# A feed-forward on Trainium2 in seven block products for eight over two token groups

## The chip, the cores and the metric

The kernel runs on one core of a Trainium2 chip. Its time is the device time of one execution in microseconds; the kernel before takes 1440.34 us (median of 3 runs, 1440.0 to 1440.73).

## What is computed

One layer for 8 samples of one token and a prompt of 1024 tokens: a mixer, attention over a memory, and a feed-forward, each added to the residual x. The change touches the feed-forward alone, with 1024 features and 4096 hidden ones, in fp32:

```python
D_MODEL, D_FF = 1024, 4096
def rmsnorm(x, g):
    xf = x.astype(jnp.float32)
    y = xf * lax.rsqrt(jnp.mean(xf * xf, axis=-1, keepdims=True) + EPS)
    return (y * g.astype(jnp.float32)).astype(x.dtype)
def ffn(x, g, w1, w2):
    h = rmsnorm(x, g) @ w1
    return jnp.square(jax.nn.relu(h)) @ w2
...
        xp = xp + mem_attend(xp, mk, mv, g_mem_x[l], mem_w_q[l], mem_g_q[l], mem_w_o[l])
        xp = xp + ffn(xp, g_ffn[l], ffn_w1[l], ffn_w2[l])
```

## The kernel before, in words

The 1032 tokens lie along the free axis in three groups of GW = 344 columns, samples first; the features lie on the partitions, 128 to a tile. XT[m] is the residual, in eight tiles. An fp32 product is made of three products in a rounded type: each operand is split into a rounded half and what is left (`halves`: a copy on ScalarE, ACT, and a subtraction on VectorE, DVE), and `dense` adds wh xh, wh xl and wl xh in PSUM on TensorE (PE).

Weights come in staged halves of 128x512 (ws, by DMAs that the queue of SyncE, SP, issues) and are split into wh and wl (`Blk`, `feed`). The framework's scheduler sets the order of every engine's queue when the program is built: by the order of the code, with splits ranked 50 instructions earlier (LIFT_W) and what empties an accumulator 600 earlier (LIFT_E). At run time each engine works through its queue in order and waits where an operand or a buffer isn't ready.

The feed-forward runs in six chunks of 6, 6, 5, 5, 5, 5 hidden tiles (CHUNKS). `ffn_up(j)` makes one hidden tile over the three groups (`f1_cell`: 24 products, then DVE multiplies max(x, 0) by 1/rms from rbf, ACT squares, ACT and DVE split into fhl). `ffn_down` takes for each of the eight output tiles m the chunk's hidden tiles (3 products each and group) and DVE adds the sum into XT[m]; in the last chunk `y_out(m)` transposes and stores the tile. The factor 1/rms is thus applied behind the products: the halves XH and XL of x carry only the gain (`norm_halves`, in `o_cell`). POOL (GpSimd) adds up the squares for the norm (`norm_sum`) and has no work afterwards. The first cells of the feed-forward stand in the code beside the memory's output products of groups 1 and 2 (`o_cells`, `up_cell`), where the streams of the memory attention run too.

Of the kernel before, what the change touches and what calls it, by code (L numbers as in the profile page):

```python
# [10 lines left out]
F32 = mybir.dt.float32  # L11
# [20 lines left out]
# SBUF slots by tag: floats per partition, count  # L32
# [11 lines left out]
# by stream: a handicap (ns) when the next one is chosen, and how much earlier its instructions rank  # L44
# [8 lines left out]
def trunk_step(ctx: ExitStack, tc: tile.TileContext, I: dict, O: list):  # L53
# [95 lines left out]
    # Ln and Tanh lie in different tables: they keep their order, with a load where they alternate  # L149
# [60 lines left out]
    def rsqrt(out, ss, scale, tmp):  # L210
        """out = (ss * scale + eps) ** -0.5, with one Newton step; tmp: a spare like out, or already the base"""
# [26 lines left out]
    def release(tag, key=None, n=1):  # L238
        """a slot is free again; with a key: once n have said so"""
# [129 lines left out]
    def halves(hi, lo, src):  # L369
        """hi = src rounded, lo = what is left"""  # L370
# [1569 lines left out]
```

## Time and profile before

| | |
|---|---|
| median of 3 runs | 1440.34 us |
| profiled execution, its span | 1436.8 us |
| PE busy | 1381.1 us (96%) |
| DVE, ACT, POOL busy | 745.2, 560.2, 101.6 us |
| DRAM read, written | 84.49 MB, 6.65 MB |

For the profiled execution the span is the only time on record: from its first to its last instruction, 3.5 us below the median of the runs. The busy times are sums over the whole span; where an engine's share is read for one stage, the table by stages is used. PE's products overlap, so their spacing, not the length of one record, tells what one costs.

### The profile page before, as it was taken

How to read it: one execution, taken by the hardware profiler on the slowest of the kernel's cores; microseconds unless marked ns; L12 is line 12 of the kernel's file. 1: busy time of each engine (PE TensorE's matmuls, PEld its weight loads, DVE VectorE, ACT ScalarE, POOL GpSimd, SP SyncE). 2: the span in 40 equal slices, each digit the busy share in tenths (PEclk: the TensorE clock that was granted, in tenths of full speed). 3: DMA queues.
4: the chain of work that ended last, by engine and by line, in shares of the span. 5: the costliest groups of instructions: out<-in, count | busy, mean ns of one | idle time of the engine just before them, and what ended most of it. 6: DMA issues, size and time to landing. Idle time of an engine off the chain costs nothing.

```text
span 1436.8 us, 22961 instructions
## 1 busy us (share of the span) xinstructions
PE 1381.1 (96%) x9029; PEld 1277.6 (89%) x9029; DVE 745.2 (52%) x1716; ACT 560.2 (39%) x1183; POOL 101.6 (7%) x137
## 2 busy tenths in 40 slices
PE   6999999999996899998899999999999999999998
PEld 5899888787886877877799999999999999999998
DVE  6276888477668664767843333333333333333331
ACT  5265465256475554565642123113212212312321
POOL 3001012300003101121300000000000000000000
PEclk9999999999997999998999999999999999999999
DMA  6014021211003444422221121111111111112032
GB/s 194 30 48 126 3 47 32 57 31 45 23 8 101 139 143 136 120 75 75 81 81 45 52 60 34 45 56 40 36 57 54 32 58 51 35 52 60 29 88 70
DMA packets 164692, 91.58 MB, mean 64 GB/s; under 512 B 24322, under 2 KB 159606, under 8 KB 164568
## 3 DMA queue, kind: packets, MB, share of 16 engines
q1 hardware_dynamic: 163944, 89.81, 21.7%
q8 instruction: 71, 1.16, 0.3%
q0 software_dynamic: 640, 0.30, 0.1%
q14 instruction: 37, 0.30, 0.1%
HBM read 84.49 MB, written 6.65 MB: 63 GB/s over the span
## 4 chain that ended last, share of the span: by engine, by line
PE 82%; DVE 10%; ACT 3%; DMA 3%; issue 1%; POOL 0%; SPq 0%; ACTq 0%; DVEq 0%; POOLq 0%
PE f L140 49%; PE win L140 8%; PE wo L140 6%; PE v L140 2%; PE gx L140 2%; PE wmo L140 1%; PE mx L140 1%; PE rgp L140 1%; DVE wl L170 1%; DMA ws<-in_w_in_dram 1%; PE go L140 1%; PE mpo L140 1%; DVE XL L181 1%; PE wq L140 1%; PE sx L140 1%
## 5 line engine op out<-in xcount | busy, mean ns | idle before, releaser
L140 PE MATMUL f<-fhl,wh 128*128 128x344 f32 x1536 | 364.8, 320 | 0.0
L160 ACT ACTIVATE wh<-ws 128x512 fp32r<-128x512 f32 (+2 forms) x292 | 159.7, 578 | 433.0 <-PE f L140 361.2
L140 PEld LDWEIGHTS f<-fhl,wh 128*128 128x128 f32 x1536 | 264.9, 188 | 0.0
L140 PE MATMUL f<-XH,wh 128*128 128x344 f32 x768 | 246.8, 321 | 2.5 <-DVE nrm L181 1.4
L140 PE MATMUL f<-XH,wl 128*128 128x344 f32 x768 | 245.6, 320 | 0.0
L140 PE MATMUL f<-fhl,wl 128*128 128x344 f32 x768 | 245.4, 320 | 0.0
L140 PE MATMUL f<-XL,wh 128*128 128x344 f32 x768 | 244.9, 319 | 0.0
L170 DVE TENSOR_TENSOR XT<-XT,f 128x344 f32<-128x344 f32 x144 | 73.8, 512 | 246.1 <-PE f L140 246.1
L170 DVE TENSOR_TENSOR wl<-ws,wh 128x512 fp32r<-128x512 f32 (+2 forms) x292 | 178.5, 639 | 31.9 <-ACT wh L160 27.4
L140 PEld LDWEIGHTS f<-XH,wh 128*128 128x128 f32 x768 | 144.4, 188 | 3.6 <-ACT wh L160 3.0
L140 PEld LDWEIGHTS f<-XH,wl 128*128 128x128 f32 x768 | 144.3, 188 | 0.3 <-issue 0.2
L140 PEld LDWEIGHTS f<-XL,wh 128*128 128x128 f32 x768 | 144.1, 188 | 0.4
L140 PEld LDWEIGHTS f<-fhl,wl 128*128 128x128 f32 x768 | 144.2, 188 | 0.0
L140 PE MATMUL win<-XL,wh 128*128 128x344 f32 x384 | 126.6, 330 | 0.0
L140 PE MATMUL win<-XH,wh 128*128 128x344 f32 x384 | 126.2, 329 | 0.2 <-ACT xy L160 0.2
L140 PE MATMUL win<-XH,wl 128*128 128x344 f32 x384 | 125.4, 327 | 0.0
L181 DVE SCALAR_TENSOR_TENSOR nrm<-f,rbf 128x344 f32<-128x344 f32 x96 | 49.4, 516 | 143.4 <-PE f L140 143.2
L160 ACT ACTIVATE nrm<-nrm 128x344 f32<-128x344 f32 x99 | 48.1, 487 | 159.1 <-DVE nrm L181 159.1
L170 DVE TENSOR_TENSOR fhl<-nrm,fhl 128x344 fp32r<-128x344 f32 x96 | 49.6, 517 | 68.6 <-ACT fhl L160 66.8
L140 PEld LDWEIGHTS win<-XL,wh 128*128 128x128 f32 x384 | 72.2, 188 | 5.2 <-issue 3.9
L140 PEld LDWEIGHTS win<-XH,wl 128*128 128x128 f32 x384 | 72.3, 188 | 3.6 <-issue 2.7
L140 PEld LDWEIGHTS win<-XH,wh 128*128 128x128 f32 x384 | 72.2, 188 | 3.3 <-issue 1.9
(427 smaller groups left out, 2105.8 us busy)
## 6 DMA issues: line engine op xcount, KB each, us to landing
ws<-in_ffn_w_dram SPq DMA_DIRECT2D x124, 256.0 KB
ws<-in_w_in_dram SPq DMA_DIRECT2D x24, 256.0 KB
ws<-in_w_out_dram SPq DMA_DIRECT2D x24, 256.0 KB
x<-in_x_prompt_dram SPq DMA_DIRECT2D x8, 512.0 KB
xr<-in_x_prompt_dram SPq DMA_DIRECT2D x16, 256.0 KB
out_dram<-yo SPq DMA_DIRECT2D x8, 512.0 KB
ws<-in_w_out_dram SPq DMA_DIRECT2D x24, 128.0 KB
ws<-in_w_out_dram SPq DMA_DIRECT2D x48, 64.0 KB
```

Source lines behind the costliest of these rows:

```text
L140: PE.matmul(out, lhsT, rhs, start=start, stop=stop)
L160: return ACT.activation(out, in_, func, **kw)
L170: return DVE.tensor_tensor(out, a, b, op=op)
L181: DVE.scalar_tensor_tensor(out, a, s, b, op0=op0, op1=op1, **kw)
```

## The change

The feed-forward is cut into 2x2 blocks of weights and two blocks of tokens (groups 0 and 1), and each 2x2 by 2x2 product is done with seven block products for eight, in Winograd's form of Strassen's method; group 2 is done in the plain way beside it, with the same weights. Sums of weight blocks (S1 to S4) and of operand blocks (T1 to T4) are made before the products and split afterwards; sums of results (U, V) behind them.

- Hidden tiles go in 16 pairs of 256. The first two pairs are plain (`pl_cell`, 12 cells of 24 products). The other 14 are `up_unit`s, 132 products each for 144.
- All of the way up comes first. Of each pair `h_done` makes nine operands (B11, B21, T1 to T4, B22, and GA, GB2 of group 2), `h_store` splits each and stores both halves to DRAM (hd): 352 KB an operand. T1, T2, T3 and T4 are sums on POOL.
- The way down is 16 `down_unit`s (8 steps of 512 hidden features by 2 halves of the output), 132 products each for 144. `h_load` fetches the operands of step c+1 while step c runs.
- `x_ready(g)` now normalises x (gain and 1/rms) before the products and splits it. `x_ops` makes T1 to T4 of x, even feature tiles on DVE, odd ones on POOL.
- XT goes to DRAM (`x_spill`) for the way up and comes back (`x_fill`), so that its place is free.
- Weights come raw (`unit_raw`, 1 MB a unit); `unit_sums` makes S1 to S4 on POOL, `prep` splits one of the eight weight operands of a unit, LOOK = 5 operands ahead of its use.
- `y_out` stands for four output tiles in the unit before the last and for four in the last one.

```diff
...
-            for k in {6: (), 7: (6, 7)}.get(m, (m,)):
-                norm_halves(k, g, GFF)
             norm_sum(m, g, NRM["f"])
+        if m == 7 and g == 0:
+            x_ready(0)
+
+    def x_ready(g):
+        with lift(LIFT_E):
+            norm_end(g, NRM["f"])
+            for m in range(8):
+                t = ring()
+                stt(t, XT[m][:, gs(g)], PRM[:, GFF + m:GFF + m + 1], NRM["f"][:, gs(g)], MUL, MUL)
+                halves(XH[:, m, gs(g)], XL[:, m, gs(g)], t)
+
+    A11, A12, S2, S1, S3, S4, A21, A22 = range(8)
+    B11, B21, T2, T1, T3, B22, T4, GA, GB2 = range(9)
...
+    def unit_sums(n):
...
+        for o, a, b, op in ((s1, a21, a22, ADD), (s2, s1, a11, SUB), (s3, a11, a21, SUB), (s4, a12, s2, SUB)):
+            POOL.tensor_tensor(o, a, b, op=op)
...
+    def prep(q):
+        n, i = divmod(q, 8)
...
+        with lift(LIFT_W):
+            if i == 0:
+                if n == 0:
+                    unit_raw(0)
+                if n + 1 < len(UNITS):
+                    unit_raw(n + 1)
+                unit_sums(n)
+            t = F("wh" if q % 2 else "wl", 1024, "wop", F32R)
...
+            halves(hi, lo, src)
+            OPS[q] = hi, lo
...
+    def h_sums(h):
+        t1, t2, t3 = HC["t"]
+        P = POOL.tensor_tensor
+        P(t1, h[0, 1], h[0, 0], op=SUB)
+        P(t3, h[1, 1], h[0, 1], op=SUB)
+        P(t2, h[1, 1], t1, op=SUB)
...
+    def h_store(p, op, src):
...
+        hi, lo = f32r(st[:, :GW]), f32r(st[:, GW:])
+        halves(hi, lo, src)
+        d = hd[p // 2].rearrange("(s o) p (q c) -> o p s q c", s=2, q=2)[op, :, :, p % 2]
+        SP.dma_start(d, st.rearrange("p (s c) -> p s c", s=2))
+
+    def h_done(p, h):
+        s = h_sums(h)
+        for op in (B11, B21, T1, T3, B22, T2, GA, GB2):
+            h_store(p, op, s[op])
+        t4 = HC["t"][1]
+        POOL.tensor_tensor(t4, h[1, 0], t4, op=SUB)
+        h_store(p, T4, t4)
...
+    def up_unit(n):
...
+        for i in range(8):
+            q = 8 * n + i
+            prep(q + LOOK)
...
+            if i == A11:
+                terms(bank(psA, "fa"), w, XOP[B11], True, False)
+                with lift(LIFT_E):
+                    act(p1, ps["fa"], AF.Copy)
+                terms(bank(psB, "fe"), w, XOP[GA][:4], True, False)
+            elif i == A12:
+                terms(ps["fa"], w, XOP[B21], False, True)
+                terms(ps["fe"], w, XOP[GA][4:], False, True)
+                with lift(LIFT_E):
+                    square_relu(h[0, 0], ps["fa"])
+                    square_relu(h[0, 2], ps["fe"])
+            elif i == S2:
+                terms(bank(psD, "fb"), w, XOP[T2], True, True)
+                with lift(LIFT_E):
+                    tt(U, ps["fb"], p1, ADD)
...
+            elif i == S4:
+                terms(bank(psD, "fg"), w, XOP[B22], True, True)
+                with lift(LIFT_E):
+                    tt(h[0, 1], ps["fg"], V, ADD)
+                act(h[0, 1], h[0, 1], AF.Relu)
+                act(h[0, 1], h[0, 1], AF.Square)
...
+        h_done(p, h)
...
+    def h_load(c, op):
+        for s, x in enumerate(h_place(c, op)):
+            SP.dma_start(x.bitcast(F32), v3(hd[c][9 * s + op], 2))
...
+    def down_unit(n):
...
+            elif i == S2:
+                banks(psD, "b")
+                for u in range(2):
+                    part("b", u, T2, True, True)
+                    add_acc(u, ps["b", u])
...
+            elif i == S1:
+                banks(psD, "c")
+                for u in range(2):
+                    part("c", u, T1, True, False)
+                    add(ms[1][u], 1, ps["c", u])
...
-    for n in CHUNKS:
-        for j in range(n):
-            if f0 or j > 2:
-                step([w1_blk(f0 + j)], ffn_up(j))
...
+    up_cell(2, 1, lambda: x_ready(2))
+    up_cell(3, 0, lambda: (x_spill(), up_rooms()))
+    up_cell(3, 1, x_ops)
+    up_cell(0, 2)
+    up_cell(1, 2, lambda: (h_done(0, PL[0]), prep(0)))
+    up_cell(2, 2, lambda: [prep(q) for q in range(1, 3)])
+    up_cell(3, 2, lambda: (h_done(1, PL[1]), [prep(q) for q in range(3, LOOK)]))
     run_steps()
+    for n, u in enumerate(UNITS):
+        if u[0] == "up":
+            up_unit(n)
+            continue
...
```

The order on the engines, at three places. First ACT in the feed-forward of before, in the middle of a chunk (nrm and fhl are a hidden tile's square and its upper half, wh a weight's):

```order
L160 ACTIVATE nrm<-nrm 128x344 [waits DVE_49]
L160 ACTIVATE fhl<-nrm 128x344 [waits Activation_49]
L160 ACTIVATE wh<-ws 128x512 [waits DMAHW1_49,PE_49]
L160 ACTIVATE wh<-ws 128x128 [waits DMAHW2_49]
L160 ACTIVATE nrm<-nrm 128x344 [waits DVE_49]
```

ACT at the change of two pairs in the middle of the way up, after (hc is a hidden tile of a pair, hst and the ring's other place wsum the store's halves, ht one of T1 to T4, wop a weight operand, gc p1's place, fa the PSUM tile of blocks A11 and A12):

```order
L160 ACTIVATE hst<-ht 128x344 [waits DMAHW4_49,Pool_49]
L160 ACTIVATE hc<-hc 128x344 [waits DVE_49]
L160 ACTIVATE hc<-hc 128x344 [waits Activation_49]
L160 ACTIVATE hst<-hc 128x344 [waits DMAHW7_49,Activation_49]
L160 ACTIVATE hc<-fe 128x344 [waits PE_49]
L160 ACTIVATE wop<-wsum 128x512
L160 ACTIVATE wsum<-hc 128x344 [waits DMAHW0_49,DVE_49]
L160 ACTIVATE wsum<-ht 128x344 [waits DMAHW1_49,Pool_49]
L160 ACTIVATE gc<-fa 128x344 [waits PE_49]
L160 ACTIVATE wop<-wraw 128x512 [waits PE_49]
```

Hidden tiles are no longer split at once: what is copied for the store are sums as well, and the copy of fa, for which PE has only done the first of its two blocks, follows on the copy of ht that waits for POOL.

POOL's last rows of before, at the end of the memory attention (rbf are the sums of squares for the norm):

```order
L1541 TENSOR_TENSOR rbf<-rbf,nrm 128x344 [waits Activation_49,Pool_49] x2
L1541 TENSOR_TENSOR rbf<-rbf,nrm 128x344 [waits Pool_49]
L1541 TENSOR_TENSOR rbf<-rbf,nrm 128x344 [waits Activation_49]
L1541 TENSOR_TENSOR rbf<-rbf,nrm 128x344 [waits Activation_49,Pool_49] x6
L1936 UNCONDITIONAL_BRANCH
```

POOL in one unit in the middle of the way up, after (L1915 to L1917 make t1, t3 and t2, L1877 the sums of weights s1, s2, s3 and s4, L1935 makes T4):

```order
L1915 TENSOR_TENSOR ht<-hc 128x344 [waits DVE_49,Activation_49]
L1916 TENSOR_TENSOR ht<-hc 128x344
L1917 TENSOR_TENSOR ht<-hc,ht 128x344 [waits Pool_49]
L1877 TENSOR_TENSOR wsum<-wraw 128x512 [waits DMAHW7_49,DMAHW0_49,DVE_49]
L1877 TENSOR_TENSOR wsum<-wsum,wraw 128x512 [waits Pool_49]
L1877 TENSOR_TENSOR wsum<-wraw 128x512 [waits DVE_49]
L1935 TENSOR_TENSOR ht<-hc,ht 128x344 [waits DVE_49,Activation_49]
L1877 TENSOR_TENSOR wsum<-wraw,wsum 128x512 [waits DVE_49,Pool_49]
```

POOL had nothing to do in the feed-forward; now each unit has eight sums there, and T4 stands behind three sums of weights for a later unit.

PE where one unit follows on another in the way up, after (fe is group 2's PSUM tile; XH and XL are x's halves):

```order
L140 MATMUL fe<-XL,wop 128x344
L140 MATMUL fe<-XH,wop 128x344 x2
L140 MATMUL fe<-XL,wop 128x344
L140 MATMUL fe<-XH,wop 128x344
L140 MATMUL fa<-XH,wop 128x344 [waits Activation_49]
L140 MATMUL fa<-XL,wop 128x344
L140 MATMUL fa<-XH,wop 128x344 x2
```

The twelve products of fe stand between the two halves of fa's sum, and the second half waits for ACT.

## Rows read from the trace of the kernel before

**Rows 1.** The page, busy time of the engines (share of the span, instructions).

```profile
PE 1381.1 (96%) x9029; PEld 1277.6 (89%) x9029; DVE 745.2 (52%) x1716; ACT 560.2 (39%) x1183; POOL 101.6 (7%) x137
```

**Rows 2.** The page, the chain that ended last: by engine, then by line.

```profile
PE 82%; DVE 10%; ACT 3%; DMA 3%; issue 1%; POOL 0%; SPq 0%; ACTq 0%; DVEq 0%; POOLq 0%
PE f L140 49%; PE win L140 8%; PE wo L140 6%; PE v L140 2%; PE gx L140 2%; PE wmo L140 1%; PE mx L140 1%; PE rgp L140 1%; DVE wl L170 1%; DMA ws<-in_w_in_dram 1%; PE go L140 1%; PE mpo L140 1%; DVE XL L181 1%; PE wq L140 1%; PE sx L140 1%
```

**Rows 3.** Table by stages: us, each engine's busy us, PEclk, DMA share, GB/s.

```profile
640.00:740.00 100.00, 89.55 (x545) 79.75 (x544) 71.39 (x153) 59.66 (x135) 16.04 (x15) 0.95 0.30 89
740.00:1374.00 634.00, 634.00 (x4037) 633.67 (x4035) 226.16 (x434) 150.30 (x314) 0.00 (x0) 1.00 0.16 46
```

**Rows 4.** The chain that ended last, in order of time: start, us, step.

```profile
727.75 644.93 PE f L140 x4101
```

**Rows 5.** Groups of VectorE, 740 to 1374 us: busy us, mean ns, idle before.

```profile
L170 DVE TENSOR_TENSOR wl<-ws,wh 128x512 fp32r<-128x512 f32 x96 | 64.2, 691 | 0.0
L170 DVE TENSOR_TENSOR XT<-XT,f 128x344 f32<-128x344 f32 x123 | 63.0, 512 | 203.4 <-PE f L140 203.4
L170 DVE TENSOR_TENSOR fhl<-nrm,fhl 128x344 fp32r<-128x344 f32 x86 | 44.5, 518 | 66.7 <-ACT fhl L160 65.2
```

**Rows 6.** Groups of ScalarE, 740 to 1374 us.

```profile
L160 ACT ACTIVATE wh<-ws 128x512 fp32r<-128x512 f32 x96 | 57.8, 628 | 328.4 <-PE f L140 328.4
L160 ACT ACTIVATE nrm<-nrm 128x344 f32<-128x344 f32 x86 | 41.9, 487 | 155.3 <-DVE nrm L181 155.3
```

**Rows 7.** Groups of POOL, whole span.

```profile
L1541 POOL TENSOR_TENSOR rbf<-rbf,nrm 128x344 f32<-128x344 f32 x21 | 23.1, 1100 | 69.5 <-ACT nrm L160 69.3
L678 POOL TENSOR_TENSOR ru<-xy 128x1032 f32<-128x1032 f32 x3 | 7.3, 2442 | 76.7 <-DVE xy L646 73.8 <-DVE XT L189 2.5 <-DMA out_dram<-rgt 0.4
```

**Rows 8.** Timeline of POOL: start, us, instruction [idle before, releaser].

```profile
599.45 1.50 POOL L1541 TENSOR_TENSOR nrm<-nrm 128x344 f32<-128x344 f32 x1 [2.53 <-ACT nrm L160]
...
659.84 0.92 POOL L1541 TENSOR_TENSOR rbf<-rbf,nrm 128x344 f32<-128x344 f32 x1 [19.28 <-ACT nrm L160]
...
708.96 2.32 POOL L1541 TENSOR_TENSOR rbf<-rbf,nrm 128x344 f32<-128x344 f32 x2 [0.64 <-ACT nrm L160]
```

**Rows 9.** Timeline of TensorE around its waits.

```profile
650.76 0.40 PE L140 MATMUL wmo<-XH,wh 128*128 128x344 f32 x1 [1.95 <-ACT wh L160]
651.00 0.32 PE L140 MATMUL wmo<-XL,wh 128*128 128x344 f32 x1
...
652.50 0.49 PE L140 MATMUL wmo<-XH,wh 128*128 128x344 f32 x1
652.79 0.49 PE L140 MATMUL wmo<-XL,wh 128*128 128x344 f32 x1
...
703.36 0.40 PE L140 MATMUL wmo<-XH,wh 128*128 128x344 f32 x1 [1.88 <-DVE nrm L181]
...
727.75 0.39 PE L140 MATMUL f<-XH,wh 128*128 128x344 f32 x1 [1.44 <-DVE nrm L181]
```

**Rows 10.** Timeline of VectorE in the stretches of rows 8.

```profile
600.20 1.12 DVE L181 SCALAR_TENSOR_TENSOR XL<-XT,PRM,XH 128x344 fp32r<-128x344 f32 x1
...
706.05 0.57 DVE L181 SCALAR_TENSOR_TENSOR XL<-XT,PRM,XH 128x344 fp32r<-128x344 f32 x1
...
708.80 1.71 DVE L181 SCALAR_TENSOR_TENSOR XL<-XT,PRM,XH 128x344 fp32r<-128x344 f32 x2
710.44 0.92 DVE L170 TENSOR_TENSOR XT<-XT,wmo 128x344 f32<-128x344 f32 x2
```

**Rows 11.** The page's DRAM traffic, and the table by stages for two early stretches.

```profile
HBM read 84.49 MB, written 6.65 MB: 63 GB/s over the span
...
5.00:10.00 5.00, 1.06 (x2) 0.00 (x0) 3.19 (x6) 4.14 (x9) 2.06 (x6) 1.00 1.14 310
15.00:20.00 5.00, 5.00 (x27) 4.78 (x26) 2.90 (x6) 0.38 (x1) 0.64 (x5) 1.00 1.01 400
```

**Rows 12.** Table by stages, the stretch of the wait at 650.76.

```profile
640.00:660.00 20.00, 18.05 (x100) 16.01 (x99) 11.94 (x26) 9.55 (x21) 0.72 (x2) 0.80 0.37 106
```

More of the change, by code (lines that the diff above doesn't have):

```diff
@@ L137, in size, with mm @@
         return n
-    def mm(out, lhsT, rhs, start=True, stop=True):
-        PE.matmul(out, lhsT, rhs, start=start, stop=stop)
+    def mm(out, lhsT, rhs, start=True, stop=True, **kw):
+        PE.matmul(out, lhsT, rhs, start=start, stop=stop, **kw)
         n = size(rhs)
@@ new lines, in unit_sums @@
+    def unit_sums(n):
+        a11, a12, a21, a22 = RAW[n]
+        k = 4 if UNITS[n][0] == "up" else 2
+        if n == 0 or UNITS[n][0] != UNITS[n - 1][0]:
+            SUM["t"] = ST["v"] if k == 4 else F("q", 2048, "wsum")
+        st = SUM["t"]
+        s1, s2, s3, s4 = (v3(st[:, 512 * j:512 * j + 512], k) for j in range(4))
+        for o, a, b, op in ((s1, a21, a22, ADD), (s2, s1, a11, SUB), (s3, a11, a21, SUB), (s4, a12, s2, SUB)):
+            POOL.tensor_tensor(o, a, b, op=op)
+        SUM[n] = {S1: s1, S2: s2, S3: s3, S4: s4, A11: a11, A12: a12, A21: a21, A22: a22}
@@ new lines, in terms, with square_relu @@
+    def terms(ps, ops, xs, first, last):
+        n = len(ops)
+        for j, ((wh, wl), (xh, xl)) in enumerate(zip(ops, xs)):
+            mm(ps, wh, xh, start=first and j == 0, stop=False, skip_group_check=True)
+            mm(ps, wh, xl, start=False, stop=False, skip_group_check=True)
+            mm(ps, wl, xh, start=False, stop=last and j == n - 1, skip_group_check=True)
+    def square_relu(o, x):
+        act(o, x, AF.Relu)
+        tt(o, o, o, MUL)
+    def h_sums(h):
[4 more added lines that the diff above has]
+        P(t2, h[1, 1], t1, op=SUB)
+        return {B11: h[0, 0], B21: h[1, 0], T2: t2, T1: t1, T3: t3, B22: h[1, 1], GA: h[0, 2], GB2: h[1, 2]}
@@ new lines, in pl_cell, with pl_new, x_spill, up_rooms @@
+    def pl_cell(f, g, b):
+        ps = psD("f1")[:, :GW]
+        dense(ps, x_terms(b, g))
+        with lift(LIFT_E):
+            square_relu(PL[f // 2][f % 2, g], ps)
+    def pl_new(p):
+        c = cells(T("qe"[p], 6 * GW, "hpl"))
+        PL[p] = {(f, g): c[3 * f + g] for f in range(2) for g in range(3)}
+    XOP = {}
+    def x_spill():
+        for m in range(8):
+            SP.dma_start(xd[m], XT[m])
+    def up_rooms():
+        drain()
+        HOP["hs"] = [F("e", 6 * GW, "xoph", F32R), F("d", 6 * GW, "xoph", F32R)]
+        HOP["ls"] = [F("d", 6 * GW, "xopl", F32R), F("q", 6 * GW, "xopl", F32R)]
+        HC["t"] = [F("ws", GW, "ht") for _ in range(3)]
+        HC["h"] = [c for i in range(2) for c in cells(F("u", 3 * GW, "hc"))]
+        HC["g"] = cells(F("g", 4 * GW, "gc"))
+        ST["v"] = F("v", 3584, "wsum")
+        room = [F("q", 2064, "hst"), ST["v"][:, 2048:]]
+        ST["ring"] = [room[i][:, 2 * GW * j:2 * GW * j + 2 * GW] for i, n in ((0, 3), (1, 2)) for j in range(n)]
+        ST["n"] = 0
@@ new lines, in x_ops, with op @@
+    def x_ops():
+        hc, lc = ([c for t in HOP[x] for c in cells(t)] for x in ("hs", "ls"))
+        g0, g1 = gs(0), gs(1)
+        for o, t in enumerate((T2, T1, T3)):
+            XOP[t] = [(hc[4 * o + k], lc[4 * o + k]) for k in range(4)]
+        XOP["12"] = XOP[T4] = [(XH[:, k, g1], XL[:, k, g1]) for k in range(4)]
+        XOP[B11] = [(XH[:, k, g0], XL[:, k, g0]) for k in range(4)]
+        XOP[B21] = [(XH[:, k, g0], XL[:, k, g0]) for k in range(4, 8)]
+        XOP[B22] = [(XH[:, k, g1], XL[:, k, g1]) for k in range(4, 8)]
+        XOP[GA] = [(XH[:, k, gs(2)], XL[:, k, gs(2)]) for k in range(8)]
+        def op(k, o, a, b, f):
+            if k % 2:
+                POOL.tensor_tensor(o, f32(a), f32(b), op=f)
+            else:
+                tt(o, f32(a), f32(b), f)
+        for k in range(4):
+            t, u = HC["g"][2 * (k % 2):2 * (k % 2) + 2]
+            (a, al), (b, bl), (c, cl), (d, dl) = (XOP[x][k] for x in (B11, "12", B21, B22))
+            op(k, t, d, b, SUB)
+            op(k, u, dl, bl, SUB)
+            op(k, t, t, u, ADD)
+            halves(*XOP[T3][k], t)
+            op(k, t, b, a, SUB)
+            op(k, u, bl, al, SUB)
+            op(k, t, t, u, ADD)
+            halves(*XOP[T1][k], t)
+            op(k, t, d, t, SUB)
+            op(k, t, dl, t, ADD)
+            halves(*XOP[T2][k], t)
+            op(k, t, c, t, SUB)
+            op(k, t, cl, t, ADD)
+            halves(*XOP[T4][k], t)
@@ new lines, in h_load, with x_fill @@
+    def h_load(c, op):
+        for s, x in enumerate(h_place(c, op)):
+            SP.dma_start(x.bitcast(F32), v3(hd[c][9 * s + op], 2))
+        HOP[c, op] = h_place(c, op)
+    def x_fill(ms):
+        if 4 in ms:
+            t = [v3(F("q", 2 * N, "XT"), 2) for _ in range(2)]
+            XT.update({m: t[m // 2 - 2][:, m % 2] for m in ms})
+        else:
+            t = v3(F("v", 3 * N, "XT"), 3)
+            XT.update({m: t[:, m] for m in range(3)})
+            XT[3] = F("u", N, "XT")
+        for m in ms:
+            SP.dma_start(XT[m], xd[m])
@@ L1884, in trunk_step, with up_cell, fn @@
         step([wcols("mem_w_q", [(0, 128 * i, 128)]) for i in range(2)], mem_q(g))
-    def up_cell(i, g):
-        step([w1_blk(i)], lambda blks: f1_cell(i, g, blks[0], g == 0))
+    def up_cell(i, g, more=None):
+        def fn(blks):
+            if g == 0 and i % 2 == 0:
+                pl_new(i // 2)
+            pl_cell(i, g, blks[0])
+            if more:
+                more()
+        step([w1_blk(i)], fn)
     def o_cells(g, ms):
@@ L1894, in trunk_step @@
         o_cells(1, ms)
-        up_cell(i, 0)
+        up_cell(i, 0, (lambda: x_ready(1)) if i else None)
     up_cell(2, 0)
```

210 lines of the change are left out of this document (167 added, 43 removed).

## The prediction

> **What bounds the kernel now.** I read the page's busy times first, then its chain of waits, then a table by stages, and only there the single groups. TensorE is busy 96% of the span [rows 1], and the chain that ended last runs on it for 82%, 49% of the span in the feed-forward's line of products [rows 2]. The table by stages says where that holds without a gap: from 740 to 1374 us PE is busy in all of the 634 us at a granted clock of 1.00, VectorE for 226 us, ScalarE for 150 and POOL not at all [rows 3]. So this stage is bound by the number of products and by nothing else. The chain gives the price of one: 644.93 us for 4101 products [rows 4], 157.3 ns. Before 740 us it is different: PE is busy 89.6 of 100 us, with the clock at 0.95. Whatever the change puts on the other engines can use their idle time, as long as nothing goes round in a ring longer than PE's own work.
>
> **What it removes.** The feed-forward has 4608 products of 128x344 before (32 up tiles of 3 groups of 24; 8 output tiles of 3 groups of 96). After: 12 plain cells of 24 (288), 14 up units of 132 and 16 down units of 132, 4248 in all. That is 360 fewer, and at 157.3 ns each **-56.6 us**, all on the path, since PE never waits there. The square and the split into halves remain; the sum of chunks into XT, 144 additions before, becomes fewer but similar ones.
>
> **Up units: the engines' sums fit, a ring does not.** One unit is 132 products, 20.8 us of PE. DVE has 8 weight splits at 0.69 us and some 17 operations of 344 columns at 0.52 [rows 5]: 14.4 us. ACT has 8 copies at 0.63 and 19 at 0.49 [rows 6]: 14.3 us. POOL has 4 sums of 344 columns and 4 of 512. For 344 columns POOL takes 1.10 us on average and for 1032 columns 2.44 [rows 7]; undisturbed it is 0.92 for 344 [rows 8]. By the slope from 0.92 to 2.44, 2.2 ns a column, I estimate 1.29 us for 512 columns; POOL then works 8.8 us. None reaches 20.8.
>
> But the queues are in order, and in ACT's the copy of fa into gc stands right behind the copy of ht, the T4 of the pair before. PE may go on adding to fa (12 products later, the second block) only when this copy has read it. POOL in turn makes T4 only after t1, t3, t2 and three weight sums, and t1 needs the square behind block S4 (fg). So, from the start of fg's last product: its record 0.32 [rows 9], addition 0.51, relu and square 0.49 each [rows 5, 6]; three sums 2.76, three weight sums 3.87, T4 0.92; T4's copy and fa's copy 0.49 each. That is 10.3 us. PE has between the end of fg and the waiting product 60 products (A21 12, A22 24, fa 12, fe 12): 9.4 us. The ring is 0.9 us longer than the work that covers it even if nothing disturbs POOL.
>
> Something does. At 708.96 two POOL sums took 2.32 us for 1.84, while two operations of VectorE took 1.71; at 599.45 one sum took 1.50 for 0.92 [rows 8], and the DVE operation at 600.20 took 1.12, where the same takes 0.57 at 706.05 [rows 10]. VectorE's additions from PSUM kept their 0.92 for two beside POOL at 710.44 [rows 10]. So sums on POOL and DVE operations with two inputs in SBUF take turns, at 0.24 to 0.58 us for each POOL sum. There are seven sums in the ring, and DVE has some ten such operations (lower halves of weights and of stored operands) in these 9 us. That adds 1.7 to 4.1 us; I take 2.4, nearer to the low end, since DVE has pauses there as well. PE then waits 3.3 us a unit. The Trainium skill, "SBUF — State Buffer", section "Who interferes with whom", says the same in a harder form: the two engines share a port pair under an exclusive lock, and an operation with two SBUF inputs blocks a GpSimd one fully. The rows agree that it is whole turns. Without that rule the ring would cost 0.9 us a unit; with every sum waiting out a whole operation, 5.0.
>
> Fourteen units; in the first three fa's copy does not stand behind T4 in ACT's order, in eleven it does: 11 x 3.3 = **+36 us** (11 x 0.9 = 10, 11 x 5.0 = 55).
>
> **Entry.** `x_ready` normalises x before the products: 8 more operations on DVE and 8 copies on ACT per group, where before the norm was put in afterwards. `x_ops` puts 20 sums on POOL (18.4 us at 0.92), 36 operations on DVE (18.7 at 0.52) and 16 copies on ACT; `h_done` of the two plain pairs 10 more POOL sums. In POOL's order 7 of x_ops' sums, 4 weight sums and 3 h sums lie between the norm of group 2 and T2, which S2 of the first unit reads: 14.4 us undisturbed, some 19 with turns. PE has behind that norm some seven plain cells of 3.8 us and then A11 and A12, 7.5 us, so over 30 us: covered. Not covered are the norm's own chain and the memory streams, which lose what the plain cells fill now; before, PE waited 1.95, 1.88 and 1.44 us at single places there [rows 9]. I take **+6 us**; those waits gone would be -5, and twice the disturbance seen before (PE idle 10.4 us in 640 to 740 [rows 3]) would be +20.
>
> **Down units.** POOL has 4 weight sums (5.2 us), DVE 8 splits and 16 additions from PSUM (13.8), ACT 8 copies, against 20.8 us. No ring passes through POOL, and additions from PSUM aren't slowed. A PSUM bank is used again six products after its last one, about the time of an addition and its record (0.83 against 0.94 us): 0 to 0.3 us a unit, 16 units, 0 to 5; **+3**.
>
> **DMA.** The up units write 9 operands of 352 KB per pair and load 1 MB of weights: 4.2 MB in 21 to 24 us, some 200 GB/s; the down units read 6.3 MB per 41 us and weights, also 200. The kernel before writes 6.65 MB in all [rows 11], so nothing there shows writes at this rate. Traffic ran at 310 to 400 GB/s in two stretches of the first 20 us [rows 11]. I take nothing, and a limit is a rival. **Tail and change-over:** two output tiles instead of one behind the last product, and a first load inside the last up unit, **+3** (1 to 5).
>
> **Sum**, on the profiled execution of 1436.8 us: -56.6 + 36 + 6 + 3 + 3 = -8.6, so 1428.2. The median of the runs is 3.5 us above that span; with the same outside it, **1432 us**. The terms' ends give 1440.3 - 56.6 + 10 - 5 + 0 + 1 = 1390 and 1440.3 - 56.6 + 55 + 20 + 5 + 5 = 1469; not all come together, so its own range is 1402 to 1458.
>
> **Rivals.**
> *The ring is hidden.* If DVE's pauses let POOL through and T4's copy comes a little sooner than I think, PE never waits in the up units: 1440.3 - 56.6 + 12 = 1396. For it: every engine's sum is below PE's. Against it: 0.9 us are missing even undisturbed, and the turns are in the trace. Chance 0.18.
> *Slower: the clock falls at each wait.* After the wait of 1.95 us at 650.76 the products' spacing went from 157 to some 286 ns [rows 9], level 1.2 instead of 2.4 GHz, and 640 to 660 shows a granted clock of 0.80 [rows 12]. A mean of 0.80 over 20 us is 8 us at half speed; I take 9, for what lies beyond 660. It loses 9 x (1 - 157/286) = 4.1 us. At each of eleven waits this is 45 us: 1432 + 45 = 1477. It decides for slower from the third fall on (8.4 us in hand, 4.1 each). Against it: after the wait of 1.44 us at 727.75 [rows 9] the clock is 1.00 from 740 on [rows 3], and in the units PE works 20 us without a gap before each wait, which it did not before 650. Chance 0.13.
> *The transfers bind.* With writes and reads mixed at 150 GB/s, an up unit takes 28 us, 7 more than PE: 14 x 7.4 = 104 less the 36 that it covers: 1500. It decides from 4.2 MB in 24 us, 175 GB/s, downwards. Nothing in the trace speaks for or against it. Chance 0.07.
> *The change doesn't do what it says.* The units change operand and PSUM bank more often than the 24 or more products in a row of before. If their spacing rose by 14 ns, 3960 of them would give back 55 us; the ring's cover grows by 60 x 14 = 0.8 us a unit, 9 in all: 1432 + 55 - 9 = 1478. Against it: a chain of 4101 products with all their changes of bank ran at 157 ns [rows 4]. Chance 0.04.
>
> **How the numbers follow.** The forecast has 0.58. 0.40 of it is faster by over 0.2% (below 1437.5; about 2.9 us, what a measurement of this kernel can tell from no change), 0.09 within it, 0.09 slower. The hidden ring adds 0.18 to faster; the clock 0.13 to slower, the transfers 0.07, the spacing 0.04. Faster 0.58, same 0.09, slower 0.33. For eight in ten the range leaves out the lower part of the hidden ring (0.08), the transfers (0.07) and the upper part of the clock's case (0.05): 1396 to 1480.
>
> **What would show it.** A profile after with PE's idle time in front of fa's products, put down to ACT's copy gc, some 3.3 us in each of eleven units that come every 24 us; POOL with its seven sums end to end there, 344 columns at 1.1 to 1.4 us, and DVE's splits over 0.8 us; a down stage with units every 20.8 us and PE full; about 200 GB/s in both; clock 1.00. I am wrong in the ring if PE waits for weights (wop) or for DMA, in the port if POOL's sums stay at 0.92, in the entry if the first up unit begins before 735 or after 765 us, and in the sign if PEclk falls below 0.95 in the up units.

## The result and the profile after

The changed kernel takes 1487.9 us (median of 4 runs, 1485.4 to 1492.6) against 1440.5: a ratio of 1.033 [1.030, 1.035]. It is 47 us slower where I forecast 8 us faster. The page after, its first busy row, its DRAM traffic and its chain (compare [rows 1, 2, 11]):

```profile
PE 1351.1 (91%) x8669; PEld 1240.6 (83%) x8669; DVE 1044.6 (70%) x2096; ACT 683.2 (46%) x1399; POOL 369.7 (25%) x341
...
HBM read 140.50 MB, written 61.60 MB: 136 GB/s over the span
...
PE 61%; DVE 15%; ACT 7%; POOL 7%; issue 5%; DMA 4%; SPq 1%; DVEq 0%; ACTq 0%; POOLq 0%
```

PE is busy 30 us less than before, not the 56.6 saved (I put the difference down to products at the lower clock and did not count them), but the span is 49 us longer: the change waits for more than it saved. The chain runs on PE for 61% where it was 82%, on POOL for 7% where it was 0%. The table by stages (us, busy us and count of PE, PEld, DVE, ACT, POOL, granted clock, DMA share, GB/s; stages: entry, the first three up units, eleven up units, the first two down units, the rest):

```profile
640.00:780.00 140.00, 104.64 (x567) 92.57 (x568) 109.70 (x208) 66.81 (x152) 45.60 (x38) 0.83 0.34 109
780.00:856.50 76.50, 65.80 (x393) 64.39 (x392) 70.51 (x94) 42.46 (x91) 41.73 (x33) 0.96 0.70 236
856.50:1117.00 260.50, 235.50 (x1454) 232.40 (x1453) 200.01 (x274) 145.41 (x296) 116.64 (x89) 0.98 0.53 188
1117.00:1178.00 61.00, 44.66 (x267) 43.63 (x266) 33.49 (x56) 15.28 (x29) 13.87 (x11) 0.86 0.87 304
1178.00:1485.90 307.90, 302.29 (x1921) 297.19 (x1920) 199.95 (x372) 77.66 (x131) 68.41 (x51) 1.00 0.53 175
```

PE never waited from 740 to 1374 us before [rows 3]; now every stage up to 1178 has gaps, and the clock is below 1.00 in all of them. The waits of PE by what ended them (us in total, times, longest):

```profile
PE fa L140 <- ACT gc L160: 33.5, 14, 3.9
PE e L140 <- DVE XT L170: 16.3, 2, 15.5
PE wmo L140 <- DVE mq L170: 11.2, 1, 11.2
...
PE nrm L140 <- POOL rbf L1541: 5.6, 2, 4.2
```

Counting products gives each stage its price. The last of the 288 plain products starts at 779.6 us; before, the 288th product of the feed-forward started at 742.8. From there 132 products of 157.3 ns are 20.76 us a unit.

| stage | forecast | measured |
|---|---|---|
| products saved | -56.6 | -56.6 |
| entry, to the last plain product | +6 | 779.6 - 742.8 = +36.8 |
| first three up units, to 856.5 | 0 | 76.9 - 62.3 = +14.6 |
| eleven up units, to 1117.1 | +36 | 260.6 - 228.4 = +32.2 |
| first two down units, to 1178.0 | part of 3 | 60.9 - 41.5 = +19.4 |
| the rest | +3 and part of 3 | +2.7 |
| sum, span against span | -8.6 | +49.1 |

### The profile page after: what moved, and what is told of

It reads as the page before. It is cut to its first block, busy times and chain, and to the rows that moved or that the text cites. A ratio compares the mean times of both kernels' runs of the same rounds, so it can differ in the third digit from the quotient of the medians.

```text
span 1485.9 us, 23738 instructions
## 1 busy us (share of the span) xinstructions
PE 1351.1 (91%) x8669; PEld 1240.6 (83%) x8669; DVE 1044.6 (70%) x2096; ACT 683.2 (46%) x1399; POOL 369.7 (25%) x341
## 4 chain that ended last, share of the span: by engine, by line
PE 61%; DVE 15%; ACT 7%; POOL 7%; issue 5%; DMA 4%; SPq 1%; DVEq 0%; ACTq 0%; POOLq 0%
PE win L140 8%; PE e L140 8%; PE wo L140 6%; PE c L140 4%; PE ga L140 4%; PE d L140 4%; PE v L140 3%; POOL wsum L1877 3%; PE fa L140 2%; PE gx L140 2%; PE b L140 2%; PE fe L140 2%; PE fd L140 2%; PE fc L140 2%; PE fb L140 2%
## 5 line engine op out<-in xcount | busy, mean ns | idle before, releaser
L140 PE MATMUL e<-XH,wop 128*128 128x344 f32 x512 | 135.1, 323 | 16.3 <-DVE XT L170 16.3
L1877 POOL TENSOR_TENSOR wsum<-wraw 128x512 f32<-128x512 f32 x60 | 86.8, 1450 | 240.9 <-DVE wop L170 178.5
L170 DVE TENSOR_TENSOR wop<-wsum,wop 128x512 fp32r<-128x512 f32 x120 | 97.2, 813 | 41.5 <-ACT wop L160 39.4
L170 DVE TENSOR_TENSOR wl<-ws,wh 128x512 fp32r<-128x512 f32 x144 | 104.5, 739 | 30.9 <-ACT wh L160 26.1
L170 DVE TENSOR_TENSOR wop<-wraw,wop 128x512 fp32r<-128x512 f32 x120 | 87.1, 727 | 54.1 <-ACT wop L160 47.9
L160 ACT ACTIVATE wh<-ws 128x512 fp32r<-128x512 f32 x144 | 88.1, 626 | 76.6 <-DMA ws<-in_w_out_dram 24.9
L140 PE MATMUL fe<-XH,wop 128*128 128x344 f32 x448 | 114.6, 319 | 0.0
L140 PEld LDWEIGHTS e<-XH,wop 128*128 128x128 f32 x512 | 91.7, 190 | 17.4 <-issue 15.7
L140 PE MATMUL e<-XL,wop 128*128 128x344 f32 x256 | 82.3, 321 | 0.0
L140 PEld LDWEIGHTS fe<-XH,wop 128*128 128x128 f32 x448 | 79.0, 188 | 0.0
```

The costliest lines, as they stand in the source:

```text
L140: PE.matmul(out, lhsT, rhs, start=start, stop=stop, **kw)
L160: return ACT.activation(out, in_, func, **kw)
L170: return DVE.tensor_tensor(out, a, b, op=op)
L1877: POOL.tensor_tensor(o, a, b, op=op)
```

## The experiments

Each kernel has one edit unless it says more. The column us is the median of all runs (2 for store_one_input and ready_moved, 10 for unlifted_no_sums, 4 for the others). "Last plain" is the start of the last plain product, "up" the time from there to the first product of the way down, "down" from there to the end, all in the one profiled execution; their sum is that execution's span, which is not the median.

| kernel | us | last plain | up | down |
|---|---|---|---|---|
| changed kernel | 1487.9 | 779.6 | 337.5 | 368.8 |
| t4_first | 1492.2 | 779.3 | 338.3 | 368.8 |
| store_late | 1461.8 | 777.7 | 308.0 | 369.9 |
| store_one_input | 1488.3 | 779.7 | 337.9 | 367.4 |
| fill_first | 1489.4 | 780.1 | 338.0 | 367.4 |
| raw_first | 1473.8 | 786.6 | 339.2 | 351.1 |
| ready_moved | 1486.6 | 775.7 | 337.7 | 368.2 |
| ready_unlifted | 1474.5 | 757.0 | 346.2 | 371.0 |
| no_x_sums | 1456.0 | 763.8 | 337.3 | 356.6 |
| unlifted_no_sums | 1439.9 | 749.5 | 333.3 | 355.0 |
| combined | 1423.0 | 756.5 | 312.5 | 351.3 |
| combined_2 | 1429.8 | 754.0 | 319.9 | 350.4 |

The first six kernels do the same work in the same order up to the last plain product, apart from a few operations at the end of it, and it starts there at 777.7 to 786.6 us: a difference of a few us in that column is not told from chance.

The theory in all but store_one_input: work that stands ahead of something in an in-order queue, not the amount of work, costs the time. The rival: VectorE, POOL and the transfers have simply too much to do.

### The ring in the way up

First the ring as the changed kernel shows it, in one unit (timelines: start, us, instruction, idle before). POOL from the first T sum to T4:

```profile
901.10 0.93 POOL L1915 TENSOR_TENSOR ht<-hc 128x344 f32<-128x344 f32 x1 [13.56 <-ACT hc L160]
901.99 1.44 POOL L1916 TENSOR_TENSOR ht<-hc 128x344 f32<-128x344 f32 x1
...
907.61 1.56 POOL L1877 TENSOR_TENSOR wsum<-wraw 128x512 f32<-128x512 f32 x1
909.13 1.19 POOL L1935 TENSOR_TENSOR ht<-hc,ht 128x344 f32<-128x344 f32 x1
```

ACT, the last three before fa's second half, and PE's first product of that half:

```profile
909.58 0.49 ACT L160 ACTIVATE hst<-hc 128x344 fp32r<-128x344 f32 x1 [1.75 <-DVE hc L170]
910.35 0.49 ACT L160 ACTIVATE hst<-ht 128x344 fp32r<-128x344 f32 x1 [0.28 <-POOL ht L1935]
910.75 0.44 ACT L160 ACTIVATE gc<-fa 128x344 f32<-128x344 f32 x1
```

```profile
911.24 0.42 PE L140 MATMUL fa<-XH,wop 128*128 128x344 f32 x1 [2.43 <-ACT gc L160]
```

The copy of fa starts as soon as T4's copy has left ACT, and PE waits 2.43 us for it. The sum at 901.10 ran undisturbed (0.93 us). The next (901.99) took 1.44: a subtraction of VectorE with two SBUF inputs had begun at 901.94, and it took 0.69.

**t4_first** puts T4 ahead of the weight sums:

```diff
-        POOL.tensor_tensor(t4, h[1, 0], t4, op=SUB)
+        mark(("T4", p), POOL.tensor_tensor(t4, h[1, 0], t4, op=SUB))
...
-            POOL.tensor_tensor(o, a, b, op=op)
+            ins = POOL.tensor_tensor(o, a, b, op=op)
+            if n >= 2 and ("T4", n) in marks and UNITS[n][0] == "up":
+                late(ins, ("T4", n))
```

> One change: on POOL the four weight sums of a later unit come behind T4 of the pair before, instead of three of them ahead of it; no other queue changes its order. Theory (the ring through POOL's and ScalarE's queues sets the pace of the way up): PE's waits in front of fa's second half, 33.5 us in the changed kernel, fall to under 8, units come every 21 us or less for 23.5, and the whole is 24 to 32 us shorter (1456 to 1464). Rival (the shared port: POOL and VectorE together can't do a unit's work in 21 us, whatever the order): the waits move to weights or to the next T sums, and the time falls by less than 10 us.

Measured: 1492.2 us, no gain; the waits before fa fell only to 26.8 us. T4 was early, as wanted, but the queue held something else. POOL, then VectorE, then ACT in one unit:

```profile
978.48 0.94 POOL L1937 TENSOR_TENSOR ht<-hc,ht 128x344 f32<-128x344 f32 x1 [1.93 <-ACT hc L160]
979.38 3.05 POOL L1877 TENSOR_TENSOR wsum<-wraw 128x512 f32<-128x512 f32 x2
```

```profile
979.72 1.60 DVE L170 TENSOR_TENSOR hc<-hc 128x344 f32<-128x344 f32 x1
```

```profile
981.35 0.49 ACT L160 ACTIVATE wsum<-hc 128x344 fp32r<-128x344 f32 x1 [1.55 <-DVE hc L170]
...
982.12 0.43 ACT L160 ACTIVATE gc<-fa 128x344 f32<-128x344 f32 x1
```

T4 is done at 979.4, and POOL goes on to the weight sums. VectorE's square of h12 (the pair's second hidden tile of group 2, operand GB2), 0.52 us by itself, waits its turn behind one of them (1.60 us), ACT's copy of h12 for the store (981.35) waits for the square, and behind it stand T4's copy and fa's. So the theory as I had put it (T4 alone) was wrong: two chains of about the same length ended ahead of fa's copy. Which of the two would be enough was not tried; the next kernel moves both.

**store_late** puts both copies behind fa's in ACT's queue:

```diff
+        HC["late"] = lambda key=None: (h_store(p, GB2, s[GB2], key), h_store(p, T4, t4, key))
...
                 with lift(LIFT_E):
-                    act(p1, ps["fa"], AF.Copy)
+                    mark(("p1", p), act(p1, ps["fa"], AF.Copy))
...
+                if "late" in HC:
+                    HC.pop("late")(("p1", p))
```

> In t4_first T4 was ready 3 us earlier and PE's waits were still 26.8 us: on ScalarE the copy of fa then stood behind the copy of h12 (the pair's last operand of group 2), whose square VectorE makes in turns with POOL. Here both copies for the store, h12's and T4's, come behind fa's copy in ScalarE's queue; POOL's order stays. Theory (fa's copy waits for whatever stands ahead of it in its queue): PE's waits in front of fa fall below 5 us, units come every 20.8 to 21.5 us, and the whole is 25 to 33 us shorter (1455 to 1463). Rival (VectorE and POOL can't do a unit's work in 21 us): units still take 23 us or more, with waits for weight operands.

POOL's order is the changed kernel's, with T4 behind the weight sums. Measured: 1461.8 us, 26 less. The way up is 29.5 us shorter, and ten units of it, the fourth to the thirteenth, run without a gap (table by stages):

```profile
855.40:1063.10 207.70, 207.70 (x1321) 207.66 (x1320) 182.74 (x250) 128.85 (x269) 109.74 (x83) 1.00 0.57 199
```

PE is busy in all of the 207.7 us, 20.77 a unit, at a clock of 1.00, and POOL, VectorE and ACT do the work they did before. So VectorE and POOL do fit in 20.8 us; the rival falls here, and the ring is shown.

**store_one_input** tests the turns between VectorE and POOL by themselves. It leaves out the subtraction in the stored lower halves.

```diff
-        halves(hi, lo, src)
+        act(hi, src, AF.Copy)
+        ts(lo, src, 0.0625)
```

> Left out: the subtraction in what is stored; the lower half is a scaled copy of the operand, one VectorE operation with one input in SBUF in the place of one with two, nine a pair. Theory (only operations with two inputs in SBUF take turns with POOL): beside them POOL's sums of 344 columns go back to 0.92 to 1.0 us (1.39 for t3, 1.18 for t2 and T4 in the changed kernel) and the ring shortens by 1 to 2 us a unit, 10 to 25 us in all. Rival (any VectorE work beside it slows POOL, or the copy blocks it too): the sums stay at 1.2 to 1.4 us and the time changes by less than 5 us.

POOL's sums t3, t2 and T4 in the changed kernel (groups from 833 to 1117 us: busy us, mean ns, idle before):

```profile
L1916 POOL TENSOR_TENSOR ht<-hc 128x344 f32<-128x344 f32 x12 | 16.7, 1392 | 0.0
L1917 POOL TENSOR_TENSOR ht<-hc,ht 128x344 f32<-128x344 f32 x13 | 15.4, 1181 | 0.0
L1935 POOL TENSOR_TENSOR ht<-hc,ht 128x344 f32<-128x344 f32 x12 | 14.0, 1168 | 1.9 <-ACT hc L160 1.9
```

The same in store_one_input, T4 first (L1936), then t2 and t3:

```profile
L1936 POOL TENSOR_TENSOR ht<-hc,ht 128x344 f32<-128x344 f32 x12 | 12.8, 1068 | 7.0 <-ACT hc L160 7.0
L1917 POOL TENSOR_TENSOR ht<-hc,ht 128x344 f32<-128x344 f32 x11 | 11.2, 1022 | 0.0
L1916 POOL TENSOR_TENSOR ht<-hc 128x344 f32<-128x344 f32 x12 | 11.1, 927 | 0.0
```

The sums went from 1.39, 1.18 and 1.17 us to 0.93, 1.02 and 1.07: beside operations with one input they are nearly undisturbed. The time did not change (1488.3), against what I expected. The build also moved one weight sum ahead of t1 on POOL, and VectorE's own work now waited for POOL instead (timelines of VectorE, then of POOL):

```profile
908.96 0.34 DVE L175 TENSOR_SCALAR hst<-hc 128x344 fp32r<-128x344 f32 x1
...
910.33 1.19 DVE L175 TENSOR_SCALAR hst<-hc 128x344 fp32r<-128x344 f32 x1 [0.19 <-DMA hd<-hst]
```

```profile
910.04 1.29 POOL L1877 TENSOR_TENSOR wsum<-wraw,wsum 128x512 f32<-128x512 f32 x1 [1.49 <-DVE wop L170]
```

The same copy takes 0.34 us at 908.96, with POOL idle, and 1.19 when POOL's sum had begun at 910.04. The turns are shown, but what they cost the whole is not separated by this run.

### The change-over

SP's queue in the changed kernel, and PE's product that waited:

```profile
1136.09 0.37 SPq L1928 DMA_DIRECT2D hd<-wsum  x1
...
1151.16 0.52 SPq L2086 DMA_DIRECT2D XL<-hd  x1
...
1155.04 3.21 SPq L2098 DMA_DIRECT2D XT<-xd  x4
```

```profile
1167.02 0.63 PE L140 MATMUL e<-XH,wop 128*128 128x344 f32 x1 [15.46 <-DVE XT L170]
```

The last fetch of the residual (XT, 1155.04) stands behind a store that waits for its data (1136.09), then loads of the next step's operands and the weights. PE's wait of 15.46 us ended when it had landed and VectorE had added; the granted clock was 0.86 over the stage, so part of it ran at 1.2 GHz.

**fill_first** fetches it right behind its other half:

```diff
-            x_fill((0, 1, 2, 3) if u[2] == 0 else (4, 5, 6, 7))
+            if u[2] == 1:
+                x_fill((4, 5, 6, 7))
+                x_fill((0, 1, 2, 3))
```

> One change: the second half of the residual is fetched from DRAM right behind the first half, ahead of the 18 loads of the next step's operands in SP's queue. Theory (PE waited 15.5 us in the second down unit because this fetch stood last in SP's queue, behind stores that wait for their data and behind 18 loads): that wait falls below 3 us, and with the clock that fell behind it the whole is 15 to 19 us shorter (1469 to 1473). Rival (the stores of the last pair and the transfers themselves bind the change-over): the fetch is early but PE waits for operands instead, and less than 6 us come back.

Measured: 1489.4, no gain. The wait of 15.46 us for XT is gone (0.46 is left); PE waits for weights and then, as I read the queue, for operands (the profile puts the second wait down to "issue"):

```profile
1169.23 0.65 PE L140 MATMUL ga<-xoph,wop 128*128 128x344 f32 x1 [8.40 <-ACT wop L160]
...
1179.78 0.46 PE L140 MATMUL ga<-XH,wop 128*128 128x344 f32 x1 [4.37 <-issue]
```

**raw_first** also has the weights of unit 16 fetched ahead of those loads:

```diff
+            if i == S1 and fetch is not None:
+                for op in (B11, GA, B21, GB2, T2, T1, T3, B22, T4):
+                    h_load(fetch, op)
...
+            if c == 1:
+                late(ins, ("raw", 16))
```

> As fill_first, where the wait for the residual went but PE then waited 8.4 us for the raw weights of the unit after, which stood behind 14 loads of operands in SP's queue. Here these weights are fetched ahead of those loads too. Theory (SP's order binds the change-over): the waits of 8.4 and 4.4 us fall below 4 in all, and the whole is 8 to 18 us shorter than the changed kernel (1470 to 1480). Rival (the transfers themselves bind: 20 MB in 60 us at 300 to 400 GB/s): PE waits for the operands of step 1 instead, and the end comes less than 5 us earlier.

Measured: 1473.8. The way down is 17.7 us shorter, all of the 19.4 but 2. By the medians the whole gained 14. In the profiled execution it gained 9.0: the entry, which the edit does not touch, took 7.0 longer and the way up 1.7. The two units took 43.4 us for 60.9 and run nearly full (table by stages):

```profile
1125.80:1169.20 43.40, 42.61 (x267) 41.61 (x267) 33.20 (x56) 15.35 (x29) 11.10 (x9) 1.00 0.91 318
```

318 GB/s moved, more than the 304 of the changed kernel, with PE busy 42.6 of 43.4 us and the clock at 1.00. The transfers don't bind; SP's order did. One repair of two shows nothing when a second wait stands right behind it.

### The entry

VectorE around PE's wait of 11.2 us, then around the norm of group 1:

```profile
647.29 1.54 DVE L181 SCALAR_TENSOR_TENSOR nrm<-XT,PRM,rbf 128x344 f32<-128x344 f32 x3
...
659.66 0.94 DVE L170 TENSOR_TENSOR mq<-wq,nrm 128x344 f32<-128x344 f32 x2
```

```profile
684.84 1.55 DVE L181 SCALAR_TENSOR_TENSOR nrm<-XT,PRM,rbf 128x344 f32<-128x344 f32 x3
...
693.80 1.64 DVE L170 TENSOR_TENSOR XL<-nrm,XH 128x344 fp32r<-128x344 f32 x2
695.36 0.16 DVE L181 SCALAR_TENSOR_TENSOR SRQ<-rscr,SRQ 128x12 f32<-128x12 f32 x1
```

PE's two longest waits in the entry, and POOL (two sums ahead of the second):

```profile
660.32 0.63 PE L140 MATMUL wmo<-XH,wh 128*128 128x344 f32 x1 [11.24 <-DVE mq L170]
...
741.09 1.51 PE L140 MATMUL nrm<-rbf,ones 128*128 128x344 f32 x2 [4.21 <-POOL rbf L1541]
```

```profile
733.66 1.38 POOL L1982 TENSOR_TENSOR gc<-XL,gc 128x344 f32<-128x344 f32 x1
734.99 6.04 POOL L1541 TENSOR_TENSOR rbf<-rbf,nrm 128x344 f32<-128x344 f32 x5
```

Three things stand in queues. `x_ready(0)` puts its multiplications and subtractions (from 647.3 on, 16 in all) ahead of the memory query's result mq (659.66), whose PSUM bank PE needs. `x_ready(1)` (684.8 to 695.4) does the same to the memory attention's statistics (SRQ, 695.36). So the attention's streams run from 700 to 724 us without a plain product among them: 120 of the 288 are done by 699, and the next stand behind group 2's output products in PE's queue. The granted clock is 0.66 from 700 to 720. And among POOL's sums of squares for group 2 stand two of `x_ops`' sums (the last at 733.66), ahead of the norm, which starts at 741.

**ready_moved** has `x_ready(0)` behind the memory query in the program; **ready_unlifted** also ranks it no earlier, in all groups:

```diff
-        if m == 7 and g == 0:
-            x_ready(0)
...
+            if g == 2:
+                x_ready(0)
...
-        with lift(LIFT_E):
+        with lift(0):
             norm_end(g, NRM["f"])
```

> Only the place of the first normalising changed: behind the memory query's product of group 2 in the program, still ranked 600 earlier. Theory (VectorE's queue order makes PE's wait of 11.2 us): that wait falls below 4 us, the last plain product comes 5 to 11 us earlier. Rival (only the rank matters): the wait stays above 8 us.

> Changed: the normalising of x stands behind the memory query's product of group 2 in the program, and is no longer ranked 600 instructions earlier, in all three groups. Theory (its chains of 9 to 11 us stood on VectorE in front of the memory query's result and of the memory attention's statistics, which PE waits for): the wait of 11.2 us at 660 goes, the last plain product (779.6 us in the changed kernel, 742.8 where the kernel before has done as many) comes 8 to 15 us earlier, and so does the end (1473 to 1480). Rival (VectorE and POOL have simply too much work in this stretch): the waits move to later ones, and the last plain product moves by less than 4 us.

ready_moved: the wait fell from 11.2 to 0.7, but one of 5.1 us for XT came in its place, and the last plain product came 4 us earlier, less than expected and hardly clear of the spread above (2 us below its lowest). ready_unlifted: 22.6 us earlier, more than expected, with 13 of it left at the end (1474.5). The streams now have plain products between them; the stretch from 700 to 720 us in the changed kernel, then here (table by stages):

```profile
700.00:720.00 20.00, 13.99 (x64) 8.81 (x64) 10.09 (x30) 11.65 (x34) 0.00 (x0) 0.66 0.22 65
700.00:720.00 20.00, 18.69 (x128) 15.64 (x127) 19.04 (x39) 14.22 (x35) 9.49 (x9) 1.00 0.49 161
```

The work is the same, so this part of the loss was order. How it divides between the three groups' ranks was not tried. Much more can't come from order alone: from 640 to 757 us VectorE is now busy 105.4 of 117 us, where the kernel before had 71.9 of 102.8 to its own 288th product. The way up grew by 8.7: in its first unit PE waits 5.0 us for a weight operand (769.92), whose copy on ACT stands behind copies of x's sums.

**no_x_sums** leaves out the sums of x (the body of `x_ops` becomes `XOP[t] = XOP[B11]`):

> Left out: the sums T1 to T4 of x (20 sums on POOL, 36 operations on VectorE, 16 copies); the products read plain blocks of x in their place. Theory (chains in queue order cost the entry, the amount of work only a part): the last plain product comes 5 to 12 us earlier and the first up unit takes 6 to 9 us less; 10 to 20 us in all. Rival (the amount of work on VectorE and POOL is the whole cost of the entry): the last plain product is back at 750 us or before, 30 us earlier.

Measured: the last plain product 15.8 us earlier and the whole 32 us less (1456.0), both more than expected. From the last plain product to the second up unit it is 26.4 us instead of 30.2, but the way up as a whole is no shorter (337.3 for 337.5). I had not expected 12 us of the gain in the way down. There the operand tiles that the sums use are free, the order of SP's queue is another, and the wait for XT is 2.9 us instead of 15.5; that the one causes the other I take from the order and have not tried by itself.

**unlifted_no_sums** has both:

> ready_unlifted and no_x_sums together (left out: the sums T1 to T4 of x). Alone they brought the last plain product from 779.6 us to 757.0 and to 763.8. Theory (the entry's loss is these two, x's norm chains ahead of others on VectorE and x's sums on VectorE and POOL): the last plain product at 741 to 748 us, as in the kernel before (742.8), and 38 to 48 us off the changed kernel's whole (1440 to 1450). Rival (each hides the same wait): 755 us or later and less than 36 us off.

749.5 us, just behind the range, and 1439.9: 48 us less, a little over the two alone (13 and 32). At the last plain product they give 30.1 together where 22.6 and 15.8 would make 38.4, so in part they hide the same wait. Of the entry's 36.8 us these two make 30.1: the place and rank of the norm chains, and x's sums with what they hold up. The other 6.7 stay open. Leaving the sums out takes away their work as well as their place in the queues, so for them order and amount are not told apart.

### Put together

**combined** is store_late, raw_first and ready_unlifted.

> store_late, raw_first and ready_unlifted together. If their gains add (25 to 33, 8 to 18, 13), 1424 to 1442, at or below the kernel before (1440.5). If the way up or the change-over is bound by the amount of work or bytes, 1455 or more.

1423.0 us, 1 below the expected range: a ratio of 0.988 [0.985, 0.990] to the kernel before, 1.2% faster than it and faster than the changed kernel. By stages of the profiled executions the gains nearly add: the entry 23.1 us (22.6 alone), the way up 25.0 (29.5), the way down 17.5 (17.7). Its busy times, and its stages of the first three units, the next eleven and the change-over:

```profile
PE 1340.4 (94%) x8669; PEld 1228.1 (86%) x8669; DVE 1041.4 (73%) x2096; ACT 677.7 (48%) x1399; POOL 368.8 (26%) x341
```

```profile
756.00:839.00 83.00, 70.36 (x403) 67.86 (x402) 76.35 (x105) 44.03 (x96) 45.88 (x36) 0.90 0.67 228
839.00:1069.00 230.00, 228.51 (x1452) 228.14 (x1451) 196.94 (x273) 141.78 (x296) 116.22 (x89) 1.00 0.60 210
1069.00:1112.40 43.40, 42.30 (x265) 41.43 (x265) 33.55 (x56) 15.34 (x29) 11.30 (x9) 1.00 0.92 325
```

The units from 839 us on and the change-over run at 1.00 with PE busy over 97%. What is left lies in the entry (13.7 us) and the first three units (82.1 us where PE alone would take 62.3): PE is busy 70 of 83 us there, VectorE 76, so there the amount of work on VectorE is not ruled out.

**combined_2** moves the plain pairs' `h_done` behind the first and second up unit:

> combined, and the sums, splits and stores of the two plain pairs stand behind the first and the second up unit instead of ahead of the first. In combined the first unit still takes 34 us. Theory (what is queued on VectorE and POOL when the first unit begins delays it): the first unit takes 22 to 27 us and the whole is 5 to 12 us shorter, 1411 to 1418. Rival (the sums of x alone hold the first unit, or the work comes back in the second and third unit): within 3 us of 1423.

1429.8, 6.8 us slower than combined (the kernel before, run beside each, was 1.7 us slower too). The first unit took 30.9 us for 33.9, but the four after it 28.3, 24.1, 24.7 and 22.8 for 24.9, 23.0, 20.8 and 20.8; the work came back, as the rival said.

## Why the prediction was wrong

**Products saved.** Right: 360 fewer, and 157 ns each wherever PE runs without a gap (PE's 12 products of one block take 1.89 us in the chain).

**The ring.** Right in its place and its owner, and near in its sum: +32.2 for +36. The sum is near in part by luck. PE's wait was 2.43 us in ten units and 0.73 in the last, 25.0 in all for the 36 of 11 x 3.3; falls of the clock, which I had as a rival, added 4.2 (below), and 3 lie in no single wait. POOL's sums of 344 columns took 0.93 to 1.44 us in the unit shown; I had 0.92 undisturbed and 1.16 to 1.50 with a turn. The rule of the Trainium skill that I had set beside it ("SBUF — State Buffer", "Who interferes with whom") agrees with the trace here: POOL's sum takes 0.93 us alone and 1.44 when VectorE's operation with two SBUF inputs had begun. I left out the copy of h12, which started only 0.8 us ahead of T4's (909.58 and 910.35), so that T4 alone gave nothing. The first three units, which I had as free, lost 14.6: fa's copy waits there too (3.9, 1.9 and 2.8 us). In the first it waits for an operation on x's sums (XL, at 785.44 on VectorE); what holds it in the other two was not tried, and store_late left all three about as they were (30.2, 23.0 and 24.5 us for 30.2, 23.0 and 23.8).

**The clock at each wait.** A rival that came true at three of eleven waits, at a third of its price. In the chain the 12 products of fa take 2.15 us mostly, and 3.5 at 886, 958 and 1030 us:

```profile
862.88 2.15 PE fa L140 x12
...
886.34 3.56 PE fa L140 x12
```

That is 1.4 us each (the granted clock is 0.57 from 886 to 890 us), against 4.1 for the long fall that I had taken the price from; it is in the 32.2. The lower level lasted longer in the entry: a granted clock of 0.83 over 140 us, of which PE was busy for 104.6.

**The entry.** This is the step that failed: +6 for +36.8, and +14.6 behind it. By my own sign for it (the first up unit not after 765 us) it had failed: that unit begins at 776.1. I weighed only POOL's part of x's sums against the plain cells and found it covered; VectorE's 36 operations for them (18.7 us) I listed and weighed against nothing, and leaving all of x's sums out brought the last plain product 15.8 us earlier. I wrote that the norm's own chain and the memory streams were not covered, and priced them by three single waits of the kernel before [rows 9]. I did not follow the chain of 16 operations through VectorE's queue, some 8 to 11 us, to ask what it now stands ahead of: the memory query's result, the attention's statistics. Without that rank and place the last plain product came 22.6 us earlier (ready_unlifted). None of the order rows ahead of the prediction shows VectorE's queue in the entry. The upper bound of 20, twice the idle time before, did not come from any row on these chains, and was too low.

**The change-over.** 19.4 for a part of 3. I priced a first load inside the last up unit, and not what stands in SP's queue ahead of the residual's fetch: stores that wait for their data, then loads. With the order changed 17.5 to 17.7 of it came back (raw_first, combined). **Transfers.** A price of 0 for them was right: 318 GB/s with PE nearly full (raw_first). The **down units** of the middle ran at 20.86 us, as forecast within 0.1 us.

My sign of a wrong direction, PEclk below 0.95 in the up units, did not show (0.96 and 0.98), and the direction was wrong all the same. The rivals that I priced for a slower result (clock, transfers, spacing) were others than the one that came. None was "work moved ahead in a queue", though my own working had found one such case in the ring.

## What to carry to other kernels

Where a change puts a chain on an engine with a high rank, follow that engine's queue from the chain on and price what now stands behind it by the whole length of the chain; an engine that has idle time left still delays everything behind it. When a repair removes the wait that the profile names and the time doesn't move, look at what stands next in the same queue: here T4 and then h12, the residual and then the weights. Here the block method's saving came through only when copies and loads for later use stood behind what the matrix engine waits for. And count the added work of every engine in the stretch where it falls: where one of them is nearly full (here VectorE, 105.4 of 117 us), a better order gives back little more.

## What the runs showed of the hardware

A VectorE operation with one SBUF input and a fixed factor, 344 columns, took 0.34 us alone and 1.19 beside a POOL sum (store_one_input), so in this case turns are not only for two inputs. The Trainium skill, "SBUF — State Buffer", "Who interferes with whom", says that such an operation can enter a mode that takes the ports shared with GpSimd; the two lengths agree with that. Loads with some stores among them ran at 318 GB/s over 43 us with PE nearly full (raw_first), which no row of the kernel before had shown.
